# Folding a norm's weight vector into the weights of the first projection of a two-layer trunk, with the start written in another order

## The chip, the cores and the metric

The kernel runs on one core of a Trainium2 chip, as one launch. The metric is the device time of that launch in microseconds; smaller is better. TensorE (PE) multiplies, its weight loads have a row of their own (PEld); VectorE is DVE, ScalarE is ACT, GpSimd is POOL, and SyncE (SP) issues nearly all transfers.

## What is computed

Two residual layers on 256 tokens of width 1024, float32 in and out. Layer 0 mixes tokens with a matrix-memory mixer, layer 1 with block-sparse attention, and each is followed by a SwiGLU block. The change touches the norm ahead of the mixer of layer 0 and the projection that reads it:

```
def rmsnorm(x, g):
    y = xf * lax.rsqrt(jnp.mean(xf * xf, axis=-1, keepdims=True) + EPS)
    return (y * g.astype(F32)).astype(x.dtype)
...
u = rmsnorm(h, norm_mix[layer])
...
q, k, v, o, gl = jnp.split(u @ w_in, [sq, 2 * sq, 2 * sq + sv, 2 * sq + 2 * sv], axis=-1)
```

In layer 0 `w_in` has 1024 rows and 3080 columns: Q and K (512 each), V and O (1024 each) and 8 gate columns. `g` scales the 1024 features, so it can be applied to `u` or to the rows of `w_in`.

## The kernel before

**Two fp16 parts.** Every float32 operand is split into a high part (rounded to fp16) and a low part (what is left). A product is three fp16 matmuls: high by high, high by low, low by high (`proj_tok`). The high part of a weight is one ACT instruction (`wh`), the low part one DVE instruction that reads the raw weight and the high part (`wl`).

**Weights.** They stream in as 1 MB tiles `raw0`, `raw1`, ... (128 partitions by 2048 columns), in the order in which they are used: `raw0`, `raw1` hold the first half of V, `raw2`, `raw3` Q, `raw4`, `raw5` K, `raw6`, `raw7` the second half of V, `raw8` to `raw11` O, `raw12` to `raw15` the output projection, and from `raw16` on the SwiGLU block. There are 5 raw buffers and 8 buffers for the parts, so a load waits until DVE has made the low parts of the tile five before it. `Weights.high` and `Weights.low` split a half tile, 1024 columns, in one instruction each (lines 283 to 298).

**Who sets the order.** Each engine runs its instructions in the order in which the program issues them (`in_queue_order`). A planner, `Pace`, keeps an estimated clock; after each matmul step `Weights.ahead` may issue one more split of each kind if it thinks that ACT or DVE is free. Ahead of that, the first projection is issued by a table written out by hand, `START` (line 62), which `start_step` (line 537) executes: `square`, `rms` (norm factor and scaled x of one of the two token tiles), `flip` (four TensorE transposes of 128 columns into a PSUM bank), `uh` and `ul` (high and low part of the transposed x, four 128-column instructions each, with the norm's weight as the per-partition scale `gmix`), `wh` and `wl` (parts of one 512-column row chunk k of `raw0` or `raw1`), `v t k` (the three matmuls of token tile t with chunk k, tile `av`), and `ahead`, from where the planner may add splits.

**After V.** V's two banks are evacuated by ACT (`vah`) and DVE (`val`). Then Q is computed for both token tiles (`aq`, 24 matmuls each); each result is copied by ACT and DVE into `n`. Then the gates, a small product (`gate`), and a chain of small steps on ACT and DVE that ends in `lf`. TensorE meanwhile runs the 24 matmuls of K for tile 0 (`ak`), then the running sum of `lf` (`pf`), three more `ak`, and then the transpose `pr` of `acol`, which DVE makes from `pf` (`fcum`, `acol`). TensorE's order is fixed, so nothing behind `pr` can start before `acol` is there.

Of the kernel before, what the change touches and what calls it, by code (L numbers as in the profile page):

```python
# [16 lines left out]
ALU = mybir.AluOpType  # L17
# [42 lines left out]


START = [
    ("square", 0), ("rms", 0), ("flip", 0, 0), ("flip", 0, 1), ("square", 1), ("gain",), ("rms", 1), ("uh", 0, 0),
# [139 lines left out]
def trunk(ctx: ExitStack, tc: tile.TileContext, a: dict, out: bass.AP):  # L203
# [16 lines left out]
    def mm(dst, lhsT, rhs, start, stop):  # L220
        nc.tensor.matmul(dst, lhsT, rhs, start=start, stop=stop)  # L221
# [36 lines left out]
    class Weights:  # L258
# [18 lines left out]
            pace.work("DMA", 0.73)  # L277
            self.landed[i] = pace.end + 2.2

        def half(self, n):  # L280
            return slice(n % 2 * 1024, (n % 2 + 1) * 1024)

        def high(self):

            i, sl = self.highs // 2, self.half(self.highs)
            if i == len(self.parts):
                self.parts.append([wpool.tile([P, 2048], F16, tag=f"w{x}", bufs=WBUFS, name=f"w{x}{i}") for x in "hl"])
            nc.scalar.activation(self.parts[i][0][:, sl], self.raws[i][:, sl], AF.Copy, scale=WS)
            self.split[self.highs] = pace.end
            self.highs += 1  # L290

        def low(self):

            i, sl = self.lows // 2, self.half(self.lows)
            h, l = self.parts[i]
            nc.vector.scalar_tensor_tensor(l[:, sl], self.raws[i][:, sl], WS, h[:, sl], op0=ALU.mult, op1=ALU.subtract)
            self.lows += 1
            self.owed += 1 - self.lows % 2

# [117 lines left out]
        nc.gpsimd.tensor_tensor(r, s1, mhalf[:, 0:1], op=ALU.pow)  # L417
        return r

    def rms(name, t, ss, engine):  # L420

        r = rms_factor(ss)
        un = act.tile([P, D], F32, tag="u", name=f"u_{name}")
        for j in range(2):
            sl = slice(j * 512, (j + 1) * 512)
            engine.tensor_scalar(un[:, sl], hres[t][:, sl], r, 1.0, op0=ALU.mult, op1=ALU.mult)
        return un

    def gain_row(src):
# [32 lines left out]
    def split_cols(dh, dl, pt, gcols, k0, t, part):  # L462

        sl = slice(t * P, (t + 1) * P)
        for i in range(4):
            src, g, h = pt[:, i * P:(i + 1) * P], gcols[:, k0 + i:k0 + i + 1], dh[:, k0 + i, sl]
            if part == "uh":
                nc.scalar.activation(h, src, AF.Copy, scale=g)
            else:
                nc.vector.scalar_tensor_tensor(dl[:, k0 + i, sl], src, g, h, op0=ALU.mult, op1=ALU.subtract)  # L470

    def flip16(dst, src):

# [61 lines left out]
    un, pts = {}, {}  # L535

    def start_step(op, *i):
        if op == "gain":
            nc.vector.tensor_scalar(gmix, gb[:, 0:KD], math.sqrt(D) * AS, None, op0=ALU.mult)
        elif op == "square":  # L540
            square_half(1, i[0], ss[1])
        elif op == "rms":
            un[i[0]] = rms(f"a{i[0]}", i[0], ss[i[0]], (nc.vector, nc.gpsimd)[i[0]])
        elif op == "flip":
            pts[i] = ybank(f"ut_a{i[0]}{i[1]}")
            transpose4(pts[i], un[i[0]][:, i[1] * 512:(i[1] + 1) * 512])
        elif op in ("uh", "ul"):
            split_cols(*u[0:2], pts[i], gmix, 4 * i[1], i[0], op)
# [143 lines left out]
    for g in range(2):  # L692
        w = ws.take_k(2, 4)
        for t in range(NT):
# [507 lines left out]
```

## Time and profile before

| | |
|---|---|
| median of 3 runs | 553.78 us (553.05 to 554.00) |
| the profiled execution | 554.33 us |
| its span in the profile | 552.6 us |
| TensorE busy | 538.5 us, 97% |
| VectorE busy | 356.1 us, 64% |
| ScalarE busy | 309.1 us, 56% |

The profiled execution is 0.55 us over the median. Busy is the share of the span in which the engine had an instruction in flight; it does not tell the clock of TensorE, which has a row of its own.

### The profile page before, as it was taken

What the parts mean: (1) busy time and instruction counts of PE and PEld (TensorE: products, weight loads), DVE (VectorE), ACT (ScalarE), POOL (GpSimd) and SP (SyncE); (2) the same over time, 40 slices, a digit from 0 to 9 for tenths busy, and PEclk for the clock granted to TensorE, in tenths of its full rate; (3) what the DMA queues carried; (4) which work ended last, traced back from release to release, by engine and by line L of the source; (5) the groups of instructions that cost most, each with busy time, mean ns of one, the idle gap of its engine ahead of it and who ended that gap; (6) DMA issues with size and microseconds to landing.
All of it is one profiled execution on the core that took longest, in us unless ns stands there. A gap on an engine that the chain in (4) does not pass through costs nothing.

```text
span 552.6 us, 7773 instructions
## 1 busy us (share of the span) xinstructions
PE 538.5 (97%) x2650; PEld 251.3 (45%) x2650; DVE 356.1 (64%) x540; ACT 309.1 (56%) x548; POOL 46.0 (8%) x105
## 2 busy tenths in 40 slices
PE   7999999999999999999999999998999999999997
PEld 3454644444444444444444445543444444444443
DVE  3888798448766556682368898857566666575701
ACT  6867784358445445471348995836546455464600
POOL 4500160010300000000012220000000000000000
PEclk8999999999999999999999999999999999999999
DMA  8999969598599878892099979737879797889602
GB/s 304 362 288 239 360 172 288 131 204 227 154 237 249 220 219 247 256 390 96 3 257 338 284 180 256 137 86 225 226 212 258 194 262 219 215 242 306 236 0 78
DMA packets 140680, 122.34 MB, mean 221 GB/s; under 512 B 66472, under 2 KB 111536, under 8 KB 140640
## 3 DMA queue, kind: packets, MB, share of 16 engines
q1 hardware_dynamic: 139904, 119.58, 76.8%
q0 software_dynamic: 736, 2.27, 1.4%
q8 instruction: 21, 0.34, 0.3%
q14 instruction: 19, 0.16, 0.1%
HBM read 106.08 MB, written 1.05 MB: 194 GB/s over the span
## 4 chain that ended last, share of the span: by engine, by line
PE 89%; DMA 3%; issue 3%; ACT 2%; DVE 1%; POOL 1%; SPq 1%; ACTq 0%; POOLq 0%; DVEq 0%
PE gu L221 38%; PE f1o L221 10%; PE f0o L221 10%; PE b L221 7%; PE ao L221 6%; PE av L221 4%; PE bv L221 4%; PE bo L221 2%; DMA u_f<-n 2%; PE ak L221 2%; PE aq L221 2%; DMA raw<-in_ffn_w_in 1%; PE s L221 1%; PE num L221 1%; PE o L221 1%
## 5 line engine op out<-in xcount | busy, mean ns | idle before, releaser
L177 DVE SCALAR_TENSOR_TENSOR wl<-raw,wh 128x1024 f16<-128x1024 f32 (+1 forms) x200 | 236.6, 1203 | 38.4 <-ACT wh L177 36.3
L177 ACT ACTIVATE wh<-raw 128x1024 f16<-128x1024 f32 (+1 forms) x200 | 201.9, 1040 | 48.6 <-DMA raw<-in_ffn_w_out 22.4
L221 PE MATMUL gu<-wh,u_f 128*128 128x512 f16 x704 | 210.1, 379 | 4.3 <-DMA u_f<-n 4.3
L221 PEld LDWEIGHTS <-u_f 128*128 128x128 f16 x1056 | 103.0, 98 | 131.6 <-DMA u_f<-n 6.3
L221 PE MATMUL gu<-wl,u_f 128*128 128x512 f16 x352 | 133.4, 379 | 1.4 <-DVE wl L177 1.4
L221 PEld LDWEIGHTS <-h 128*128 128x128 f16 x528 | 51.7, 98 | 62.3
L177 DVE SCALAR_TENSOR_TENSOR fh<-gu,fsg 128x256 f32<-128x256 f32 x44 | 18.6, 423 | 54.2 <-ACT fsg L177 54.1
L177 ACT ACTIVATE fsg<-gu 128x256 f32<-128x256 f32 x44 | 16.8, 382 | 63.3 <-PE gu L221 63.3
L221 PE MATMUL f0o<-wh,h 128*128 128x512 f16 x176 | 46.6, 379 | 0.0
L221 PE MATMUL f1o<-wh,h 128*128 128x512 f16 x176 | 46.6, 379 | 0.0
L221 PEld LDWEIGHTS <-u_a 128*128 128x128 f16 x336 | 29.2, 99 | 34.9 <-ACT u_a L177 1.9
L221 PEld LDWEIGHTS <-u_b 128*128 128x128 f16 x288 | 27.8, 98 | 32.8 <-issue 1.0
L221 PE MATMUL b<-wh,u_b 128*128 128x512 f16 x128 | 38.9, 379 | 0.0
L177 ACT ACTIVATE junk<-x 128x512 f32<-128x512 f32 x16 | 10.1, 630 | 41.6 <-DVE x L177 39.3
L221 PE MATMUL f1o<-wl,h 128*128 128x512 f16 x88 | 27.5, 379 | 0.0
L221 PE MATMUL f0o<-wl,h 128*128 128x512 f16 x88 | 27.4, 379 | 0.0
L177 DVE TENSOR_TENSOR n<-fh,n 128x256 f16<-128x256 f32 x44 | 18.6, 422 | 10.7 <-ACT n L177 10.7
L221 PE MATMUL b<-wl,u_b 128*128 128x512 f16 x64 | 24.3, 379 | 0.7 <-DVE wl L177 0.7
L177 ACT ACTIVATE n<-fh 128x256 f16<-128x256 f32 x44 | 18.0, 409 | 11.9 <-DMA u_f<-n 5.9
L221 PE MATMUL av<-wh,u_a 128*128 128x512 f16 x64 | 21.8, 403 | 1.7 <-ACT u_a L177 1.7
L177 POOL TENSOR_TENSOR r<-s,mhalf 128x1 f32<-128x1 f32 x8 | 4.9, 609 | 212.9 <-DVE s L177 212.9
L221 PE MATMUL bv<-wh,u_b 128*128 128x512 f16 x64 | 20.0, 379 | 0.0
(178 smaller groups left out, 470.6 us busy)
## 6 DMA issues: line engine op xcount, KB each, us to landing
raw<-in_ffn_w_in SPq DMA_DIRECT2D x176, 256.0 KB, 4.4
raw<-in_ffn_w_out SPq DMA_DIRECT2D x88, 256.0 KB, 5.2
raw<-in_a_w_in SPq DMA_DIRECT2D x48, 256.0 KB, 5.4
raw<-in_b_w_in SPq DMA_DIRECT2D x48, 256.0 KB, 5.4
raw<-in_a_w_out SPq DMA_DIRECT2D x16, 256.0 KB, 5.7
raw<-in_b_w_out SPq DMA_DIRECT2D x16, 256.0 KB, 5.2
grow<-in_norm_ffn POOLq DMA_DIRECT2D x2, 512.0 KB, 6.6
out<-x SPq DMA_DIRECT2D x4, 256.0 KB, 2.1
```

The costliest lines, as they stand in the source:

```text
L177: return fn(*args, **kw)
L221: nc.tensor.matmul(dst, lhsT, rhs, start=start, stop=stop)
```

## The change

The scale `gmix` of the norm's weight leaves the split of x and enters the split of the weights. x is now split with a constant, so that one instruction covers 512 columns (4 x 128) where four did. Every weight tile of the layer's input projection (`raw0` to `raw11`) is split with `gmix[:, k]`, which differs from chunk to chunk, so a half tile of 1024 columns takes two instructions of 512 on ACT and two on DVE. The gate columns are multiplied by the gain first. The table `START` is written anew: token tile 0 goes first, six zero matmuls (`warm`) are put between the first steps, the scaling of token tile 1 moves from POOL to DVE, and `ahead` stands four steps of V from the end where it stood seven.

```
 START = [
-    ("square", 0), ("rms", 0), ("flip", 0, 0), ("flip", 0, 1), ("square", 1), ("gain",), ("rms", 1), ("uh", 0, 0),
+    ("square", 0), ("rms", 0), ("flip", 0, 0), ("flip", 0, 1), ("warm", 1), ("gain",), ("uh", 0, 0), ("wh", 0), ("ul", 0, 0), ("wl", 0),
...
-        def half(self, n):
-            return slice(n % 2 * 1024, (n % 2 + 1) * 1024)
+        def rows(self, n):
+
+            i, h = n // 2, n % 2 * 1024
+            if i >= 12:
+                return [(slice(h, h + 1024), WS)]
+            k = i % 2 * 4 + n % 2 * 2
+            return [(slice(h + j * 512, h + (j + 1) * 512), self.gains[:, k + j:k + j + 1]) for j in range(2)]
...
-            nc.scalar.activation(self.parts[i][0][:, sl], self.raws[i][:, sl], AF.Copy, scale=WS)
+            for sl, scale in self.rows(self.highs):
+                nc.scalar.activation(self.parts[i][0][:, sl], self.raws[i][:, sl], AF.Copy, scale=scale)
...
-            nc.vector.scalar_tensor_tensor(l[:, sl], self.raws[i][:, sl], WS, h[:, sl], op0=ALU.mult, op1=ALU.subtract)
+            for sl, scale in self.rows(self.lows):
+                nc.vector.scalar_tensor_tensor(l[:, sl], self.raws[i][:, sl], scale, h[:, sl], op0=ALU.mult, op1=ALU.subtract)
...
-            engine.tensor_scalar(un[:, sl], hres[t][:, sl], r, 1.0, op0=ALU.mult, op1=ALU.mult)
+            nc.vector.tensor_scalar(un[:, sl], hres[t][:, sl], r, 1.0, op0=ALU.mult, op1=ALU.mult)
...
-        for i in range(4):
-            src, g, h = pt[:, i * P:(i + 1) * P], gcols[:, k0 + i:k0 + i + 1], dh[:, k0 + i, sl]
-            if part == "uh":
-                nc.scalar.activation(h, src, AF.Copy, scale=g)
-            else:
-                nc.vector.scalar_tensor_tensor(dl[:, k0 + i, sl], src, g, h, op0=ALU.mult, op1=ALU.subtract)
+        h, l = (d[:, k0:k0 + 4, t * P:(t + 1) * P] for d in (dh, dl))
+        v = pt.rearrange("p (k n) -> p k n", k=4)
+        c = math.sqrt(D) * AS
+        if part == "uh":
+            nc.scalar.activation(h, v, AF.Copy, scale=c)
+        else:
+            nc.vector.scalar_tensor_tensor(l, v, c, h, op0=ALU.mult, op1=ALU.subtract)
...
-            nc.scalar.activation(w[k][0], raw, AF.Copy, scale=WS)
+            nc.scalar.activation(w[k][0], raw, AF.Copy, scale=gmix[:, k:k + 1])
...
-            nc.vector.tensor_scalar(gmix, gb[:, 0:KD], math.sqrt(D) * AS, None, op0=ALU.mult)
+            nc.vector.tensor_scalar(gmix, gb[:, 0:KD], WS, None, op0=ALU.mult)
+            ws.gains = gmix
+        elif op == "warm":
+            for _ in range(i[0]):
+                mm(warm, zero16[:, 0:P], zero16, True, True)
...
-                nc.vector.tensor_scalar(gh, gr, WS, None, op0=ALU.mult)
-                nc.vector.scalar_tensor_tensor(gl, gr, WS, gh, op0=ALU.mult, op1=ALU.subtract)
+                nc.vector.tensor_tensor(gr, gr, gmix.unsqueeze(2).to_broadcast([P, KD, 8]), op=ALU.mult)
+                nc.vector.tensor_copy(gh, gr)
+                nc.vector.tensor_tensor(gl, gr, gh, op=ALU.subtract)
```

What this does to the queues is seen at three places. The first is ACT from its first weight split to the second token tile, before and in the change (`u16_a` is the split x, `ut_a` the transposes, `junk` the squares of x).

```order
L177 ACTIVATE wh0_126<-raw0_88 128x512
L177 ACTIVATE junk_143,ss_133<-x1_84 128x512
L177 ACTIVATE junk_162,ss_133<-x1_84 128x512
L177 ACTIVATE u16_a_125<-ut_a00_152,cols_mix_141 128x128 x4
L177 ACTIVATE wh0_126<-raw0_88 128x512 x3
L177 ACTIVATE u16_a_125<-ut_a10_184,cols_mix_141 128x128 x4
```

```order
L177 ACTIVATE u16_a_125<-ut_a00_149 128x4x128
L177 ACTIVATE wh0_126<-raw0_88,cols_mix_136 128x512
L177 ACTIVATE u16_a_125<-ut_a01_154 128x4x128
L177 ACTIVATE wh0_126<-raw0_88,cols_mix_136 128x512
L177 ACTIVATE junk_174,ss_133<-x1_84 128x512
L177 ACTIVATE junk_176,ss_133<-x1_84 128x512
L177 ACTIVATE wh0_126<-raw0_88,cols_mix_136 128x512 x2
L177 ACTIVATE wh1_128<-raw1_94,cols_mix_136 128x512
L177 ACTIVATE u16_a_125<-ut_a10_201 128x4x128
```

The squares of token tile 1 have moved behind the first two weight chunks, and both halves of token tile 0 stand ahead of them. The second place is TensorE at the same point, as a difference: two `warm` matmuls take the place of the transposes of token tile 1, which now stand behind the fourth step of V.

```order
-L459 MATMUL ut_a_184<-ident,u_a_169 128x128 x4
-L459 MATMUL ut_a_189<-ident,u_a_169 128x128 x4
+L221 LDWEIGHTS zero_77
+L221 MATMUL warm<-zero_77 128x512
+L221 LDWEIGHTS zero_77
+L221 MATMUL warm<-zero_77 128x512
```

Behind the V product TensorE's instructions stand in the same order as before to the end. The third place is DVE from the evacuation of V to the copy of the second Q tile (`n16<-aq1`), before and in the change.

```order
L177 SCALAR_TENSOR_TENSOR wl2_270<-raw2_99,wh2_269 128x1024 x2
L177 SCALAR_TENSOR_TENSOR wl3_284<-raw3_104,wh3_283 128x1024
L177 SCALAR_TENSOR_TENSOR val_335<-av00_130,vah_334 128x512
L177 SCALAR_TENSOR_TENSOR val_335<-av01_131,vah_334 128x512
L177 SCALAR_TENSOR_TENSOR wl3_284<-raw3_104,wh3_283 128x1024
L177 SCALAR_TENSOR_TENSOR wl4_300<-raw4_109,wh4_299 128x1024 x2
L177 SCALAR_TENSOR_TENSOR n16_400<-aq0_358,n16_400 128x512
L177 TENSOR_SCALAR gh_347<-gr_305 128x64
L177 SCALAR_TENSOR_TENSOR gl_348<-gr_305,gh_347 128x64
L177 SCALAR_TENSOR_TENSOR wl5_381<-raw5_256,wh5_380 128x1024 x2
L177 SCALAR_TENSOR_TENSOR wl6_398<-raw6_261,wh6_397 128x1024
L177 SCALAR_TENSOR_TENSOR n16_445<-aq1_406,n16_445 128x512
```

```order
L177 SCALAR_TENSOR_TENSOR wl2_261<-raw2_99,cols_mix_136,wh2_260 128x512 x2
L177 SCALAR_TENSOR_TENSOR val_310<-av00_130,vah_309 128x512
L177 SCALAR_TENSOR_TENSOR val_310<-av01_131,vah_309 128x512
L177 SCALAR_TENSOR_TENSOR wl2_261<-raw2_99,cols_mix_136,wh2_260 128x512 x2
L177 SCALAR_TENSOR_TENSOR wl3_335<-raw3_104,cols_mix_136,wh3_334 128x512 x4
L177 SCALAR_TENSOR_TENSOR n16_381<-aq0_344,n16_381 128x512
L177 TENSOR_TENSOR gr_280<-gr_280,cols_mix_136 128x64
L177 CAST gh_322<-gr_280 128x64
L177 TENSOR_TENSOR gl_323<-gr_280,gh_322 128x64
L177 SCALAR_TENSOR_TENSOR wl4_367<-raw4_109,cols_mix_136,wh4_366 128x512 x4
L177 SCALAR_TENSOR_TENSOR wl5_398<-raw5_247,cols_mix_136,wh5_397 128x512 x4
L177 SCALAR_TENSOR_TENSOR n16_438<-aq1_388,n16_438 128x512
```

Three half tiles were split ahead of `val` before, one is now; between the two copies of Q there are four half tiles where there were three.

## Rows read from the trace of the kernel before

**Rows 1.** The page, its parts 1 and 2: TensorE's busy time, its granted clock

```profile
PE 538.5 (97%) x2650; PEld 251.3 (45%) x2650; DVE 356.1 (64%) x540; ACT 309.1 (56%) x548; POOL 46.0 (8%) x105
...
PEclk8999999999999999999999999999999999999999
```

**Rows 2.** Stretches of the start: length, busy us (instructions) per engine, PEclk, DMA share, GB/s

```profile
5.70:9.00 3.30, 1.56 (x10) 1.01 (x10) 1.01 (x4) 2.16 (x6) 0.16 (x1) 1.00 1.03 398
9.10:15.80 6.70, 6.45 (x18) 2.77 (x19) 5.84 (x17) 6.02 (x19) 6.37 (x12) 0.50 1.05 390
```

**Rows 3.** Timeline of the start, TensorE, POOL, DVE: start, us, instruction, [idle before <-releaser]

```profile
5.29 0.57 POOL L177 TENSOR_TENSOR r<-s,mhalf 128x1 f32<-128x1 f32 x1 [3.76 <-DVE s L177]
5.78 0.39 PE L221 MATMUL warm<-zero 128*128 128x512 f16 x1
5.89 0.88 DVE L177 TENSOR_SCALAR u_a<-x,r 128x512 f32<-128x512 f32 x2 [0.69 <-POOL r L177]
6.43 1.09 PE L459 MATMUL ut_a<-ident,u_a 128*128 128x128 f32 x8 [0.26 <-DVE u_a L177]
...
9.22 0.61 PE L221 MATMUL av<-wh,u_a 128*128 128x512 f16 x1 [1.70 <-ACT u_a L177]
...
24.22 0.38 PE L221 MATMUL aq<-wh,u_a 128*128 128x512 f16 x1
```

**Rows 4.** The chain that ended last, after V: start, us, what

```profile
24.39 10.36 PE aq L221 x48
```

**Rows 5.** Timeline of the weight loads of TensorE at `pr`

```profile
42.35 0.09 PEld L653 LDWEIGHTS pr<-ident,acol 128*4 128x4 f32 x2 [0.49 <-DVE acol L177]
```

**Rows 6.** Timeline of DVE from the evacuation of V to `acol`

```profile
25.05 1.29 DVE L177 SCALAR_TENSOR_TENSOR val<-av,vah 128x512 f16<-128x512 f32 x2 [1.63 <-ACT vah L177]
26.26 3.48 DVE L177 SCALAR_TENSOR_TENSOR wl<-raw,wh 128x1024 f16<-128x1024 f32 x3
30.23 0.69 DVE L177 SCALAR_TENSOR_TENSOR n<-aq,n 128x512 f16<-128x512 f32 x1 [0.49 <-ACT n L177]
...
31.20 3.49 DVE L177 SCALAR_TENSOR_TENSOR wl<-raw,wh 128x1024 f16<-128x1024 f32 x3
35.41 0.69 DVE L177 SCALAR_TENSOR_TENSOR n<-aq,n 128x512 f16<-128x512 f32 x1 [0.72 <-ACT n L177]
...
38.53 3.49 DVE L177 SCALAR_TENSOR_TENSOR wl<-raw,wh 128x1024 f16<-128x1024 f32 x3
41.94 0.16 DVE L177 COPY fcum<-pf 128x8 f32<-128x8 f32 x1
42.13 0.17 DVE L177 TENSOR_TENSOR acol<-gate,fcum 128x8 f32<-128x8 f32 x1
```

**Rows 7.** Timeline of ACT in the start

```profile
7.44 0.63 ACT L177 ACTIVATE junk<-x 128x512 f32<-128x512 f32 x1 [0.77 <-DMA x<-in_x]
...
8.82 1.12 ACT L177 ACTIVATE u_a<-ut_a,cols_mix 128x128 f16<-128x128 f32 x4
9.82 1.68 ACT L177 ACTIVATE wh<-raw 128x512 f16<-128x512 f32 x3
...
24.42 1.09 ACT L177 ACTIVATE vah<-av 128x512 f16<-128x512 f32 x2 [2.23 <-PE av L221]
```

**Rows 8.** Groups by form, whole span: constant or per-partition scale; xcount | busy us, mean ns

```profile
L177 DVE SCALAR_TENSOR_TENSOR u_f<-x,r,grow 128x512 f32<-128x512 f32 x4 | 2.8, 749 | 1.3 <-POOL r L177 1.3
...
L177 DVE SCALAR_TENSOR_TENSOR n<-u_f,n 128x512 f16<-128x512 f32 x4 | 2.7, 692 | 0.1
```

**Rows 9.** The same view for ACT

```profile
L177 ACT ACTIVATE n<-fh 128x256 f16<-128x256 f32 x44 | 18.0, 409 | 11.9 <-DMA u_f<-n 5.9 <-DVE fh L177 5.3 <-DMA h<-n 0.7
...
L177 ACT ACTIVATE p<-p,rsm 128x256 f16<-128x256 f32 x8 | 4.2, 530 | 0.0
```

**Rows 10.** TensorE's waits over the span: us in total, times, longest

```profile
PE gu L221 <- DMA u_f<-n: 4.3, 4, 1.9
PE av L221 <- ACT u_a L177: 1.7, 1, 1.7
```

More of the change, by code (lines that the diff above doesn't have):

```diff
@@ L278, in quarter @@
             self.landed[i] = pace.end + 2.2
-        def half(self, n):
-            return slice(n % 2 * 1024, (n % 2 + 1) * 1024)
+        def rows(self, n):
[4 more added lines that the diff above has]
+            return [(slice(h + j * 512, h + (j + 1) * 512), self.gains[:, k + j:k + j + 1]) for j in range(2)]
         def high(self):
-            i, sl = self.highs // 2, self.half(self.highs)
+            i = self.highs // 2
             if i == len(self.parts):
                 self.parts.append([wpool.tile([P, 2048], F16, tag=f"w{x}", bufs=WBUFS, name=f"w{x}{i}") for x in "hl"])
-            nc.scalar.activation(self.parts[i][0][:, sl], self.raws[i][:, sl], AF.Copy, scale=WS)
+            for sl, scale in self.rows(self.highs):
+                nc.scalar.activation(self.parts[i][0][:, sl], self.raws[i][:, sl], AF.Copy, scale=scale)
             self.split[self.highs] = pace.end
@@ L292, in low @@
         def low(self):
-            i, sl = self.lows // 2, self.half(self.lows)
+            i = self.lows // 2
             h, l = self.parts[i]
-            nc.vector.scalar_tensor_tensor(l[:, sl], self.raws[i][:, sl], WS, h[:, sl], op0=ALU.mult, op1=ALU.subtract)
+            for sl, scale in self.rows(self.lows):
+                nc.vector.scalar_tensor_tensor(l[:, sl], self.raws[i][:, sl], scale, h[:, sl], op0=ALU.mult, op1=ALU.subtract)
             self.lows += 1
@@ L418, in rms_factor, with rms @@
         return r
-    def rms(name, t, ss, engine):
-        r = rms_factor(ss)
+    def rms(name, t, r):
         un = act.tile([P, D], F32, tag="u", name=f"u_{name}")
@@ L460, in transpose4, with split_cols @@
         pace.spend(0.44)
-    def split_cols(dh, dl, pt, gcols, k0, t, part):
-        sl = slice(t * P, (t + 1) * P)
-        for i in range(4):
-            src, g, h = pt[:, i * P:(i + 1) * P], gcols[:, k0 + i:k0 + i + 1], dh[:, k0 + i, sl]
-            if part == "uh":
-                nc.scalar.activation(h, src, AF.Copy, scale=g)
-            else:
-                nc.vector.scalar_tensor_tensor(dl[:, k0 + i, sl], src, g, h, op0=ALU.mult, op1=ALU.subtract)
+    def split_cols(dh, dl, pt, k0, t, part):
+        h, l = (d[:, k0:k0 + 4, t * P:(t + 1) * P] for d in (dh, dl))
[5 more added lines that the diff above has]
+            nc.vector.scalar_tensor_tensor(l, v, c, h, op0=ALU.mult, op1=ALU.subtract)
     def flip16(dst, src):
@@ L523, in split_chunk @@
         if op == "wh":
-            nc.scalar.activation(w[k][0], raw, AF.Copy, scale=WS)
+            nc.scalar.activation(w[k][0], raw, AF.Copy, scale=gmix[:, k:k + 1])
         else:
-            nc.vector.scalar_tensor_tensor(w[k][1], raw, WS, w[k][0], op0=ALU.mult, op1=ALU.subtract)
+            nc.vector.scalar_tensor_tensor(w[k][1], raw, gmix[:, k:k + 1], w[k][0], op0=ALU.mult, op1=ALU.subtract)
     ss = [new_ss(t) for t in range(NT)]
-    for n in range(2):
-        square_half(0, n, ss[0])
-    split_chunk(0, "wh")
     gb, gmix = gain_cols("mix", rows_mix, KD)
@@ L534, in trunk @@
         mm(warm, zero16[:, 0:P], zero16, True, True)
-    un, pts = {}, {}
+    un, pts, factor = {}, {}, {}
     def start_step(op, *i):
         if op == "gain":
-            nc.vector.tensor_scalar(gmix, gb[:, 0:KD], math.sqrt(D) * AS, None, op0=ALU.mult)
+            nc.vector.tensor_scalar(gmix, gb[:, 0:KD], WS, None, op0=ALU.mult)
[3 more added lines that the diff above has]
+                mm(warm, zero16[:, 0:P], zero16, True, True)
         elif op == "square":
-            square_half(1, i[0], ss[1])
+            for n in range(2):
+                square_half(i[0], n, ss[i[0]])
         elif op == "rms":
-            un[i[0]] = rms(f"a{i[0]}", i[0], ss[i[0]], (nc.vector, nc.gpsimd)[i[0]])
+            factor[i[0]] = rms_factor(ss[i[0]])
+            if i[0] == 0:
+                un[0] = rms("a0", 0, factor[0])
+        elif op == "scale":
+            un[1] = rms("a1", 1, factor[1])
         elif op == "flip":
@@ L547, in start_step @@
         elif op in ("uh", "ul"):
[L548 removed]
+            split_cols(*u[0:2], pts[i], 4 * i[1], i[0], op)
         elif op in ("wh", "wl"):
```

10 rows, old and new, of the table START are left out of this document.

## The prediction, made before the changed kernel had run

> **What bounds the kernel.** I read the page first: TensorE is busy for 97% of the span, and only the first of its 40 slices shows a clock under full speed [rows 1]. A time saved elsewhere is therefore worth nothing unless TensorE waits for it, and whatever TensorE gains or loses at one place it carries to the end, as long as nothing later absorbs it. Next I read its waits: there are few, the longest 1.9 us on the transposed norm of a SwiGLU block, and 1.7 us in the start for the split of x [rows 10]. Then the start itself. The zero matmul at 5.78 takes 0.39 us and the granted clock is 1.00 until 9.0; TensorE then stands still from the transposes (6.43 to 7.52) to 9.22, and from 9.1 to 15.8 it is granted half, 1.2 GHz [rows 2, 3]. So the V product runs cold for two thirds of its time and the first matmul of Q comes at 24.22 [rows 3]. From there 48 matmuls of Q take 10.36 us, 0.216 each, with no wait [rows 4], and TensorE goes on so past `pr`. That is the place to look at: the weight load of `pr` waited 0.49 us for `acol` and got it just as the matmuls ahead of it ended [rows 5]. DVE's queue thus already arrives at 42.35 with no slack, though TensorE does not yet stand still for it.
>
> **The start.** Prices: an ACT instruction of 512 columns out of PSUM takes 0.60 and the next starts after 0.49 (two in 1.09), a weight chunk of 512 after 0.53 (three in 1.68) [rows 7]. The chunk now has a per-partition scale. On ACT a 256-column instruction with one takes 530 ns, one with a constant 409 [rows 9]; I take 0.10 more per instruction, 0.63 from start to start, because the two rows differ by 0.12 but read different tiles. The Trainium skill (ScalarE: Activation LUTs, What ACT_TABLE_LOAD costs) says that each per-partition pointer operand adds about 93 ns, which speaks against the change; by it the five pointer splits ahead of the second token tile would cost 0.03 us less in all than by my 0.10.
>
> The first four transposes are done at about 7.05 (half of 1.09 from 6.43, and the tail) [rows 3]. ACT then runs: `uh` 7.05 to 7.65, first chunk to 8.3, `uh` to 8.8, second chunk to 9.4, the two squares of tile 1 (1.38 from 7.44 to the next instruction at 8.82 [rows 7]) to 10.8, third chunk to 11.4, fourth to 12.05. DVE follows: third low part 11.5 to 12.15, then the scaling of tile 1 (its factor is ready at 11.7, after POOL's 0.57; two instructions take 0.88 [rows 3]) to 13.0, fourth low part to 13.7. TensorE finishes the fourth step of tile 0 at 14.15 and transposes tile 1; the first half is there at 14.75, its high part at 15.4, its low part at 16.15, the step that needs it ends at 16.4. Eleven steps of three matmuls at 0.216 follow: V ends at 23.5 where it ended at 24.22. **Gain of the start: 0.7 us.** The six zero matmuls, 1.3 us at full clock, lie in gaps in which TensorE waits for the splits; without that cover they would cost 1.3. The clock moves this sum less than it seems, since up to the fourth step TensorE waits for splits at either clock. If it stayed at half from 9.1 to 15.8 as before, the last two matmuls of that step would cost 0.4 more and the transposes 0.5, and V would end at 24.4; I take full clock and keep this for the upper end.
>
> **After V.** Here the change takes more than it gave. Prices on DVE: 512 columns with a constant, 0.605 from start to start (`val`: two from 25.05 to 26.26); 1024 columns, 1.137 (three from 38.53 to 41.94) [rows 6]. A per-partition scale: 749 against 692 ns at 512 columns [rows 8], so 0.06 more, 0.665 per new split and 1.33 per half tile. No row shows this very form. From below the scale could be free, 0.605; from above it could cost what it does on ACT, 0.12 [rows 9], so 0.725. I take 0.665, since rows 8 are the same engine and size.
>
> `val` started 0.83 after Q's first matmul (25.05 against 24.22) because the last step of V was tile 0's; now tile 0 ends one step, 0.65, earlier. So `val` starts at 23.5 + 0.18 = 23.7. Behind it stand two halves of `raw3`'s and one of `raw2`'s low parts that Q itself needs, six splits: 23.7 + 1.21 + 6 x 0.665, and 0.08 for the last one's end, gives 28.98. TensorE, at Q since 23.5, cannot run its last step of tile 0 before that; two more matmuls end at 29.46. Before, 24 of them ended at 24.22 + 5.18 = 29.40. **The gain of the start is gone at the end of the first Q tile.** DVE's copy of it comes 0.84 later as before (30.23 against 29.40 [rows 6]): 30.30. From its start to the next split 0.97 us went by (30.23 to 31.20); a third small gate instruction makes it 1.17 (0.2, as from `fcum` to `acol` [rows 6]). With 8 x 0.665 = 5.32 the copy of the second Q tile starts at 36.79. Before it started at 35.41, after 0.72 of idling. All the small gate steps stand behind it, 3.12 us from there to 38.53 [rows 6]; then six splits, 3.99, where three of 1024 took 3.41. `acol` is 1.38 + 0.58 = **2.0 us later** than before, at about 44.1. TensorE reaches `pr` at the same time as before and now waits for it. Everything behind stands in the same order, so TensorE carries the 2.0 to the end.
>
> Check of the other parts. ACT has 20 splits of 0.63 between the first `val` and `pr`, 12.6 us of some 20, and each high part is needed only when DVE comes to it, at 0.665 apiece; I count nothing. Transfers: the buffer of `raw2` comes free at 26.3 and no longer ahead of `val`, so `raw7` is loaded later, but its second half is split only behind `pr`. There 18 splits, to the end of `raw11`, cost DVE 0.1 us more each than half of a 1024-column one, 1.7 us in all. TensorE has moved 2.0 back by then, and I count nothing for it; if that cover is gone, it costs up to 1.7 where the scores of the heads wait for DVE. The scaling of tile 1 leaves POOL, which nobody waits for afterwards.
>
> **Sum.** -0.7 in the start, +2.7 from there to `pr`: +2.0. Against the profiled execution, 554.33, that is 556.3; that execution was 0.55 over the median of the runs, so I forecast **555.8 us** for the median.
>
> **Rivals.** (1) The DVE queue keeps up, and the change is faster. It needs `acol` 1.1 us earlier than before. Even with V at 23.0 and the first `val` at 23.2 that is 2.6 us less from there than I count, or 20 splits at 0.54 instead of 0.665. The bare rate of the columns is 1.137 - 0.605 = 0.53 per 512, so the fixed part and the scale would both have to vanish; that is the point from which it decides. For it speaks that rows 8 are not weight splits; against it, `val`. Its time is that of the start's gain with V ending between 23.0 and 23.5: 0.7 to 1.2 less, 552.6 to 553.1. Chance 0.12. (2) DVE is late, but less: a free scale and V at 23.0 (ACT's scale free too) give 0.5 less for `val` and 20 x 0.06 less behind it, `acol` 0.3 late: 554.1; with 1.0 late, 554.8. Chance 0.23. (3) The clock or a second wait adds to it. The clock fell after a gap of 1.7 us once, and stayed low for 6.7 us [rows 2, 3]. If it does that again where TensorE transposes tile 1 or stands at `pr`, half a stretch of that length costs 1.7 more: 557.5. Against it: the wait of 1.9 us on the norms [rows 10] left the clock at full [rows 1]. Or DVE, dearer by 1.7 up to `raw11`, holds up the heads. Chance 0.15. (4) The forecast, 554.9 to 557: chance 0.50.
>
> **How the numbers follow.** A measurement of this kernel can tell about 0.2%, 1.1 us, from no change: 552.7 to 554.9. Faster: rival 1, 0.12. The same: rival 2, 0.23. Slower: the forecast and rival 3, 0.65. The range leaves out most of rival 1 and the end of rival 3: **553.0 to 557.8**. The forecast's own range is 554.9 to 557.
>
> **What would show it.** In the changed profile: V ends near 23.5 with no stretch, or a shorter one, at half clock; a 512-column low part of `raw2` or later at about 0.665 from start to start; TensorE waits of a few tenths in Q's first tile for `wl`; the copy of the second Q tile on DVE behind `wl` and not behind ACT; a TensorE wait of about 2 us at `pr` for `acol`, which is a new row among its waits; the remaining waits as before. I am wrong if `pr` waits for nothing, if DVE's splits come at 0.57 or less, or if V ends before 22.5.

## The result, and the profile after

| | before | changed |
|---|---|---|
| median | 553.48 us (5 executions, 552.44 to 554.00) | 557.41 us (5 executions, 556.15 to 558.64) |
| ratio | | 1.0076, 95% interval 1.0054 to 1.0099 |
| the profiled execution, its span | 554.33, 552.6 us | 556.15, 554.2 us |

The change makes the kernel slower, by 0.5 to 1.0% (by 0.3 to 0.7% when it was measured again, experiment 1). Between the two profiled executions the difference is 1.8 us, between the medians 3.9; where the rest comes from is told below. The page, parts 1 and 2, of the changed kernel:

```profile
PE 537.9 (97%) x2656; PEld 251.0 (45%) x2656; DVE 360.5 (65%) x551; ACT 313.7 (57%) x556; POOL 43.3 (8%) x103
...
PEclk9999999999999999999999999999999999999999
```

TensorE's busy time is the same [rows 1]; the first of the 40 slices now shows full clock. In the stretches of the start:

```profile
5.70:9.00 3.30, 2.50 (x12) 1.40 (x13) 2.12 (x5) 1.79 (x4) 0.16 (x1) 1.00 1.02 366
9.10:15.80 6.70, 5.13 (x24) 2.37 (x23) 4.14 (x8) 4.17 (x10) 4.43 (x10) 1.00 1.05 387
```

The half clock of the second stretch [rows 2] is gone, yet TensorE is less busy there: it waits. The timeline of the start and of `pr` (start, us, instruction, [idle before <-releaser]):

```profile
6.44 1.17 PE L465 MATMUL ut_a<-ident,u_a 128*128 128x128 f32 x8
...
11.60 0.75 DVE L177 SCALAR_TENSOR_TENSOR wl<-raw,cols_mix,wh 128x512 f16<-128x512 f32 x1 [0.40 <-ACT wh L177]
11.79 1.11 POOL L580 DMA_DIRECT2D gr<-in_a_w_in  x1
12.27 1.24 DVE L177 TENSOR_SCALAR u_a<-x,r 128x512 f32<-128x512 f32 x2
13.44 0.74 DVE L177 SCALAR_TENSOR_TENSOR wl<-raw,cols_mix,wh 128x512 f16<-128x512 f32 x1
14.22 0.38 PE L221 MATMUL av<-wl,u_a 128*128 128x512 f16 x1 [0.80 <-DVE wl L177]
14.65 1.03 PE L465 MATMUL ut_a<-ident,u_a 128*128 128x128 f32 x8
...
16.53 0.96 DVE L177 SCALAR_TENSOR_TENSOR wl<-raw,cols_mix,wh 128x512 f16<-128x512 f32 x1
16.67 0.60 PE L221 MATMUL av<-wh,u_a 128*128 128x512 f16 x2
...
24.02 0.38 PE L221 MATMUL aq<-wh,u_a 128*128 128x512 f16 x1
...
26.25 0.38 PE L221 MATMUL aq<-wl,u_a 128*128 128x512 f16 x1 [0.56 <-DVE wl L177]
...
44.95 0.38 PE L665 MATMUL pr<-ident,acol 128*4 128x128 f32 x2 [2.00 <-DVE acol L177]
```

V ends at 24.02, only 0.2 earlier than before [rows 3]. TensorE waits 0.56 in Q's first tile for a low part and 2.00 at `pr`, where before had no wait at either place. The queue that it waits for is DVE's:

```profile
24.20 1.34 DVE L177 SCALAR_TENSOR_TENSOR val<-av,vah 128x512 f16<-128x512 f32 x2 [2.38 <-ACT vah L177]
25.46 4.06 DVE L177 SCALAR_TENSOR_TENSOR wl<-raw,cols_mix,wh 128x512 f16<-128x512 f32 x6
30.83 0.69 DVE L177 SCALAR_TENSOR_TENSOR n<-aq,n 128x512 f16<-128x512 f32 x1 [1.31 <-ACT n L177]
...
32.05 5.38 DVE L177 SCALAR_TENSOR_TENSOR wl<-raw,cols_mix,wh 128x512 f16<-128x512 f32 x8
37.35 0.68 DVE L177 SCALAR_TENSOR_TENSOR n<-aq,n 128x512 f16<-128x512 f32 x1
...
40.47 4.06 DVE L177 SCALAR_TENSOR_TENSOR wl<-raw,cols_mix,wh 128x512 f16<-128x512 f32 x6
44.45 0.16 DVE L177 COPY fcum<-pf 128x8 f32<-128x8 f32 x1
44.64 0.17 DVE L177 TENSOR_TENSOR acol<-gate,fcum 128x8 f32<-128x8 f32 x1
```

Against [rows 6]: six splits stand between `val` and the first copy, eight between the copies, with no idling ahead of the second copy, and `acol` comes 2.5 later. The 2.38 us that DVE idles ahead of `val` are no relief, because the splits that are missing later stand behind `val`. The groups by form, and TensorE's waits over the span (us in total, times, longest):

```profile
L177 DVE SCALAR_TENSOR_TENSOR wl<-raw,cols_mix,wh 128x512 f16<-128x512 f32 x48 | 33.5, 758 | 0.4 <-ACT wh L177 0.4
...
L177 ACT ACTIVATE wh<-raw,cols_mix 128x512 f16<-128x512 f32 x48 | 30.6, 715 | 0.0
```

```profile
PE gu L221 <- DMA u_f<-n: 3.3, 3, 1.8
PE pr L665 <- DVE acol L177: 2.0, 1, 2.0
...
PE aq L221 <- DVE wl L177: 0.6, 1, 0.6
```

The bill: `pr` runs 2.6 us later (44.95 against 42.36, which is 0.01 behind the weight load of [rows 5]), but the span is only 1.6 longer. The missing 1.0 is the wait that left the first row: three waits of 3.3 us where [rows 10] had four of 4.3. It is this one of the kernel before, on the norm of layer 0's SwiGLU block, shown with SyncE's two transposes that it waits for:

```profile
111.67 6.58 SPq L474 DMA_TRANSPOSE u_f<-n  x2
...
119.32 0.39 PE L221 MATMUL gu<-wh,u_f 128*128 128x512 f16 x1 [1.05 <-DMA u_f<-n]
```

In the changed kernel the same two transposes take 1.05 less, and TensorE does not wait:

```profile
114.27 5.53 SPq L480 DMA_TRANSPOSE u_f<-n  x2
```

The other part of the median's difference is the clock. Of the changed kernel's twelve executions in this and the next run, the eight with a mean granted clock of 0.999 or 1.00 took 555.64 to 557.10, the four with 0.996 or 0.997 took 557.41 to 558.64.

### The profile page after: what moved, and what is told of

Same layout as the page of the kernel before. It is cut to its first block, busy times and chain, and to the rows that moved or that the text cites. A ratio compares the mean times of both kernels' runs of the same rounds, so it can differ in the third digit from the quotient of the medians.

```text
span 554.2 us, 7778 instructions
## 1 busy us (share of the span) xinstructions
PE 537.9 (97%) x2656; PEld 251.0 (45%) x2656; DVE 360.5 (65%) x551; ACT 313.7 (57%) x556; POOL 43.3 (8%) x103
## 3 DMA queue, kind: packets, MB, share of 16 engines
HBM read 106.08 MB, written 1.05 MB: 193 GB/s over the span
## 4 chain that ended last, share of the span: by engine, by line
PE 85%; DMA 5%; DVE 4%; issue 2%; ACT 2%; SPq 1%; POOL 0%; DVEq 0%; ACTq 0%; POOLq 0%
PE gu L221 37%; PE f1o L221 10%; PE f0o L221 10%; PE b L221 7%; PE ao L221 6%; PE bv L221 4%; PE av L221 3%; PE bo L221 2%; DVE wl L177 2%; DMA u_f<-n 2%; DMA x<-in_x 1%; DMA raw<-in_ffn_w_in 1%; PE s L221 1%; PE ak L221 1%; PE num L221 1%
## 5 line engine op out<-in xcount | busy, mean ns | idle before, releaser
L177 DVE SCALAR_TENSOR_TENSOR wl<-raw,wh 128x1024 f16<-128x1024 f32 x172 | 207.5, 1221 | 36.5 <-ACT wh L177 34.4
L177 ACT ACTIVATE wh<-raw 128x1024 f16<-128x1024 f32 x172 | 178.6, 1059 | 47.3 <-DMA raw<-in_ffn_w_in 25.5
L177 DVE SCALAR_TENSOR_TENSOR wl<-raw,cols_mix,wh 128x512 f16<-128x512 f32 x48 | 33.5, 758 | 0.4 <-ACT wh L177 0.4
L177 ACT ACTIVATE wh<-raw,cols_mix 128x512 f16<-128x512 f32 x48 | 30.6, 715 | 0.0
```

The source lines that it names most:

```text
L177: return fn(*args, **kw)
```

## The experiments

The kernels ran in three groups (experiments 1 to 4, 5 to 8 and 9 to 12), each beside the kernel before on the same chip, whose medians were 553.82, 553.93 and 553.66 us (30, 23 and 35 executions). Two stretches of each profiled execution tell the kernels apart better than the whole time does: from the first transposes to Q's first matmul (A), and from there to `pr` (B). Where `pr` was moved back, six matmuls are 1.3 us and nine 1.9 us of B. B repeats: it is 20.92 or 20.93 in the five profiles that have the changed kernel's splits in their places (the changed kernel twice, experiments 2, 8 and 12). A repeats less well, because the clock falls in some starts: the fold alone and the fold with `pr` later have the same start and differ by 0.77.

| kernel | median, us (executions) | ratio to before, 95% | A | B | waits in B |
|---|---|---|---|---|---|
| before | 553.48 (5) | | 17.79 | 18.14 | none |
| changed | 557.41 (5) | 1.0054 to 1.0099 | 17.58 | 20.93 | 0.56, 2.00 |
| changed, again | 556.25 (7) | 1.0028 to 1.0068 | 17.50 | 20.93 | 0.6, 1.99 |
| `pr` nine matmuls later | 555.18 (12) | 1.0008 to 1.0039 | 17.88 | 20.92 | 0.6 |
| 1024 columns, constant | 554.74 (12) | 1.0011 to 1.0042 | 17.84 | 19.44 | 1.03 |
| 512 columns, constant | 555.20 (12) | 1.0018 to 1.0049 | 17.55 | 19.94 | 0.5, 1.15 |
| fold alone | 553.82 (12) | 0.9992 to 1.0023 | 16.75 | 18.98 | 0.84 |
| order alone | 556.62 (6) | 1.0031 to 1.0067 | 18.61 | 19.36 | 1.03 |
| low parts of Q earlier | 554.38 (12) | 0.9996 to 1.0026 | 17.42 | 19.19 | 1.04 |
| no zero matmuls | 558.17 (6) | 1.0056 to 1.0102 | 17.72 | 20.93 | 0.6, 1.99 |
| fold, `pr` later | 553.21 (12) | 0.9970 to 1.0006 | 17.52 | 19.27 | none |
| fold, zero matmuls, `pr` later | 553.22 (12) | 0.9954 to 0.9998 | 16.52 | 19.27 | none |
| low parts earlier, `pr` later | 554.64 (12) | 0.9988 to 1.0030 | 17.81 | 19.28 | none |
| POOL's DMA issues later | 556.93 (12) | 1.0025 to 1.0065 | 17.31 | 20.92 | 0.6, 1.99 |

**1. The changed kernel again.**

> The changed kernel once more, unchanged, for a second trace beside the runs below. If the time lost is a queue of fixed length on DVE, the wait of TensorE for acol at pr is 2.0 us again within 0.2, and the time lies between 556 and 559. If the spread of the five runs seen (556.2 to 558.6) is TensorE's clock, this trace shows a stretch at half clock in the start or behind pr whenever its time is over 557; if it is the transposes of the norm ahead of the SwiGLU block, it shows a wait of about 1 us for u_f at the second token tile, which the first trace of this kernel did not have.

A, B and both waits come back to within 0.1 us, and the wait at `u_f` is missing again. Only one of its seven executions had the lower clock, which fits the median, 1.2 us lower. Where the slower executions lose their time this run could not tell, since the profiled one took 556.27.

**2. `pr` later**: `"cm"`, the planner's delay ahead of `pr`, 5.47 to 7.6.

> Only pr moves: nine matmuls of K (1.9 us) later in TensorE's order. Theory, DVE's queue is late at acol: TensorE has work in that time, the wait of 2.0 us at pr shrinks to under 0.2, and the time falls by 1.8 to 2.0 against the changed kernel. Rival, the wait only moves (to the mask of the decay or to the heads behind): a new wait of 1 to 2 us further on and the same time within 0.5. Rival, TensorE's clock falls because of the stand at pr: the time falls by 3 or more, and no run has a clock under 0.999.

B is the same 20.92 with nine matmuls of K more in it: the 2.00 us at `pr` are filled with work. The wait was thus a real stop and not work that would have been done anyway. Of the executions at 0.999 or 1.00 the median is 554.5 (7), against 556.2 of the eight of the changed kernel: 1.7 of the 2.0 come through. Between the medians of all executions it is 1.1, because five of the twelve had a clock of 0.996 or 0.997, with no wait at `pr`. The profiled execution was one of these (557.31). It lost some 1.7 us behind the norm of layer 1, where the clock falls to half from the matmul on that follows a wait of 1.95 us (0.67 over the four microseconds shown, 0.90 over the next four):

```profile
388.00:392.00 4.00, 2.82 (x8) 1.02 (x8) 2.25 (x5) 2.37 (x4) 0.00 (x0) 0.67 0.96 226
```

In the changed kernel's own profile the wait there is 1.85 and the clock stays at 1.00. In the start of this profile, too, TensorE is slow: its matmuls take 0.57 to 0.63 us up to 10.06, where the changed kernel's take 0.38, although the granted clock reads 1.00 there.

**3. and 4. The price of a split, in two steps.** Both leave the norm's weight out of Q, K, O and the second half of V. The third splits these tiles in 1024 columns with a constant, the fourth in 512 with a constant:

```
-            if i >= 12:
+            if i >= 2:
```

```
-            return [(slice(h + j * 512, h + (j + 1) * 512), self.gains[:, k + j:k + j + 1]) for j in range(2)]
+            return [(slice(h + j * 512, h + (j + 1) * 512), WS) for j in range(2)]
```

> From raw2 on, the weights are split as before the change: one instruction of 1024 columns with a constant; this leaves the gain out of Q, K, O and the second half of V. The new START stays. Theory, DVE's queue: 20 splits at 0.665 become 10 at 1.137, 1.9 us less up to acol; the wait at pr is 0.3 or less, Q's first tile waits less, and the time is 1.5 to 2 us under the changed kernel. Rival, the new order of the start is what costs: the wait at pr stays over 1.5 us and the time changes by less than 0.5.

> From raw2 on, 512 columns per split as in the changed kernel, but with a constant in place of the gain (the gain is left out of Q, K, O and the second half of V). It parts the two prices: the scale, 0.06 per split by the rows, and the second instruction. Theory: a split takes 0.605 from start to start, 20 of them 1.2 us less, the wait at pr is 0.8 and the time 1.2 under the changed kernel. If the scale is free, the wait stays at 2.0; if the scale is all of the price, it falls by 1.9.

In the fourth, DVE's order is that of the changed kernel, and only the scale differs (timeline of DVE, the six splits ahead of `acol`, and ACT's group of splits):

```profile
39.91 3.69 DVE L177 SCALAR_TENSOR_TENSOR wl<-raw,wh 128x512 f16<-128x512 f32 x6
43.52 0.16 DVE L177 COPY fcum<-pf 128x8 f32<-128x8 f32 x1
...
L177 ACT ACTIVATE wh<-raw 128x512 f16<-128x512 f32 x40 | 21.7, 620 | 0.1
```

3.61 for six is 0.602 a split, against (44.45 - 40.47) / 6 = 0.663 in the changed kernel: the per-partition scale costs DVE 0.061 us. The fourteen splits behind the first copy make 0.85 of it, and the wait at `pr` falls by 0.85, from 2.00 to 1.15; I had expected 0.8, from all twenty splits, but ahead of the first copy DVE idles in both kernels. With 1024 columns the rest goes as well, but TensorE then waits 1.03 in Q's first tile, not less than 0.56 as I had it, since three half tiles of low parts that Q needs still stand behind `val`. So the price of the split explains the wait at `pr`, and not the whole of B: 1.3 of the 2.8 us are left at the old price.

**5. and 6. Either half alone.** The fold with the start in the old order (tile 1 scaled on POOL, no zero matmuls); and the new order without the fold (x split in four instructions with the scale, weights in 1024 columns with a constant):

```
+    ("square", 0), ("rms", 0), ("flip", 0, 0), ("flip", 0, 1), ("gain",), ("wh", 0), ("square", 1), ("rms", 1), ("scale", 1), ("uh", 0, 0),
+    ("wl", 0), ("ul", 0, 0), ("v", 0, 0), ("flip", 1, 0), ("flip", 1, 1), ("wh", 3), ("wh", 1), ("wh", 2),
...
+            un[1] = rms("a1", 1, factor[1], nc.gpsimd)
```

```
-            if i >= 12:
+            if i >= 2:
...
+        for i in range(4):
+            src, g, h = pt[:, i * P:(i + 1) * P], gcols[:, k0 + i:k0 + i + 1], dh[:, k0 + i, sl]
```

> The fold of the norm's weight and the 512-column splits alone; the start keeps the order of before (no zero matmuls among its steps, tile 1 scaled on POOL, the first weight chunk's high part behind the weight vector that it now needs). My theory (the price is DVE's: 20 splits with a per-partition scale between Q's first matmul and the weight load of pr): the last step of V is tile 0's again, so val starts some 0.8 us behind Q's first matmul as in before, but every 512 columns cost 0.66 where 1024 cost 1.14, so acol is late and TensorE waits at pr, by 0.6 to 1.5 us, since before had 0.49 and 0.72 us of idle DVE to use up; time 0.3 to 1.0 us over before. Rival, the order of the start is what costs: no wait at pr, time within 0.3 us of before or below it.

> The new order of the start alone: zero matmuls among its steps, tile 1 scaled on DVE, V's steps in the new order; the gain stays in the columns of x (four 128-column instructions) and the weights are split in 1024 columns with a constant. My theory: with four small instructions per half of x instead of one, V ends about 1 us later than in the changed kernel, 24.7 to 25.5; val comes early behind Q's first matmul, so that the second tile of low parts stands in front of nothing at pr: wait at pr 0 to 0.3, a wait of up to 1 us in Q's first tile for a low part; time 554.5 to 555.8, 1 to 2 over before, from the start. Rival, the order of the start is what the wait at pr comes from (val ahead of the second half tiles): a wait of 1 us or more at pr with 1024-column splits too, time over 556.

Stretch of the start and timeline of TensorE, the fold alone:

```profile
9.10:15.80 6.70, 6.00 (x23) 2.87 (x23) 5.63 (x9) 5.78 (x12) 6.03 (x11) 0.75 1.05 391
...
23.14 0.38 PE L221 MATMUL aq<-wh,u_a 128*128 128x512 f16 x1
...
42.12 0.38 PE L665 MATMUL pr<-ident,acol 128*4 128x128 f32 x2 [0.84 <-DVE acol L177]
```

and the order alone:

```profile
9.10:15.80 6.70, 5.48 (x21) 2.26 (x20) 5.14 (x13) 4.09 (x11) 3.72 (x8) 0.75 1.05 391
...
25.01 0.38 PE L221 MATMUL aq<-wh,u_a 128*128 128x512 f16 x1
...
27.72 0.38 PE L221 MATMUL aq<-wl,u_a 128*128 128x512 f16 x1 [1.03 <-DVE wl L177]
...
44.37 0.38 PE L665 MATMUL pr<-ident,acol 128*4 128x128 f32 x2
```

The fold alone costs nothing (553.82 against 553.93): it pays 0.84 at `pr`, as my theory had it, but V ends earlier, which I had not counted, and `pr` runs 0.24 sooner than before. Two things go with the earlier end of V, and no run takes them apart: the shorter split of x, and a clock that is at half for a shorter time (0.75 on average over the stretch of [rows 2], where before has 0.50). The order alone gives nearly the whole loss, 556.62 against 553.93: A is 0.8 longer, then 1.03 in Q's first tile for a low part behind `val`. Its profile, too, has 0.75 in that stretch. At most 0.4 of the 0.8 is the clock's, since the low part that the fourth step needs is ready only at 14.62 and its matmul ran at 15.01; and its two executions with a clock of 0.999 or 1.00 still took 555.88. The rival's wait at `pr` did not come: there the order alone has none. Its wait is the one in Q's first tile. Summed over A and B of these profiles, against before: fold -0.2, order +2.0, both +2.6; with the A of 17.52 that the same start has in experiment 9, the fold would be +0.6, so that the sum is good to some 0.8 only. In these profiles the rest, 0.7, lies in B: the dearer splits cost 0.84 there in the old order and 1.57 in the new one, with more of them behind `val`.

**7. The low parts of Q earlier.** The parts of V's last two chunks stand ahead of tile 0's fifth step, and the planner may begin eight steps of V before the end (not seven, as the expectation below says) instead of four:

```
-    ("wl", 5), ("v", 0, 4), ("v", 1, 3), ("v", 1, 4), ("wh", 6), ("wl", 6), ("v", 0, 5), ("v", 1, 5), ("wh", 7), ("wl", 7),
-    ("ahead",), ("v", 0, 6), ("v", 1, 6), ("v", 0, 7), ("v", 1, 7),
+    ("wl", 5), ("wh", 6), ("wl", 6), ("wh", 7), ("wl", 7), ("v", 0, 4), ("ahead",), ("v", 1, 3), ("v", 1, 4), ("v", 0, 5), ("v", 1, 5),
+    ("v", 0, 6), ("v", 1, 6), ("v", 0, 7), ("v", 1, 7),
```

> The changed kernel with one thing moved: the high and low parts of V's last two chunks stand earlier in the start, and the step that starts Q's low parts stands seven steps of V ahead of the end instead of four, so DVE has three half tiles of low parts done before val (it idled 2.38 us there) and six splits instead of eight between the two copies of Q. My theory (DVE's queue behind val is what costs, and its order decides, not the price of a split): the wait of 0.56 in Q's first tile is gone, the wait at pr falls from 2.0 to between 0 and 0.7, time 1.3 to 2.5 us under the changed kernel at the same clock, 553.8 to 555.0. Rival, the price of the splits alone decides, wherever they stand: the wait at pr stays above 1.3 and the time within 0.7 us of the changed kernel's.

Timelines of DVE and TensorE:

```profile
24.14 1.28 DVE L177 SCALAR_TENSOR_TENSOR val<-av,vah 128x512 f16<-128x512 f32 x2
...
42.97 0.38 PE L665 MATMUL pr<-ident,acol 128*4 128x128 f32 x2 [1.04 <-DVE acol L177]
```

DVE's idling ahead of `val` is gone, and so are the wait in Q's first tile and half of that at `pr` (more is left than the 0.7 that I expected at most). With the same number of splits at the same price B falls by 1.7, and the kernel is level with before. The rival, that the price alone decides wherever the splits stand, falls.

**8. No zero matmuls** among the steps of the start (the four `warm` entries of the table taken out).

> The changed kernel without the six zero matmuls between the steps of the start. My theory: they lie in TensorE's waits, so taking them out gives back no time in itself, but TensorE then stands still between the first transposes and the first step of V and again for the splits, and the granted clock falls to half there as it did in before (9.1 to 15.8); V ends 0.5 to 1.0 us later (24.5 to 25.0), the wait at pr shrinks by as much as DVE is early, so that the time moves by 0 to 0.6 us only. Rival 1: the clock stays at full without them, V ends within 0.2 of 24.02, no change in time. Rival 2: they stand in TensorE's way, V ends earlier by 0.2 or more.

My theory was wrong and the first rival right for the start: the clock stays at full there and A is 17.72, so in this profile the zero matmuls neither cost nor gave anything. The time is not lower, though. The profile has half clock at another place, right behind the wait at `pr`:

```profile
44.00:46.00 2.00, 0.89 (x6) 0.53 (x7) 1.21 (x5) 2.00 (x4) 0.00 (x0) 1.00 0.49 187
46.00:50.00 4.00, 4.00 (x12) 1.48 (x11) 3.80 (x9) 2.13 (x4) 0.00 (x0) 0.57 0.55 113
```

The changed kernel, with the same wait:

```profile
44.00:46.00 2.00, 1.05 (x6) 0.60 (x7) 1.20 (x4) 2.00 (x4) 0.00 (x0) 1.00 0.51 192
46.00:50.00 4.00, 4.00 (x20) 1.85 (x19) 3.80 (x9) 2.04 (x5) 0.00 (x0) 1.00 0.57 118
```

Twelve matmuls in four microseconds instead of twenty are 8 x 0.216 = 1.7 us. Five of the six executions had a mean clock of 0.993 to 0.996; the one at 0.999 took 555.56. Five of six against four of twelve of the changed kernel is too few to say that the zero matmuls make such a fall rarer.

**9. to 11. A better version.** `"cm"` at 6.6 puts `pr` six matmuls later: on the fold with the old order, on the same with eight zero matmuls behind the first transposes, and on the seventh kernel.

```
-    ("square", 0), ("rms", 0), ("flip", 0, 0), ("flip", 0, 1), ("gain",), ("wh", 0), ("square", 1), ("rms", 1), ("scale", 1), ("uh", 0, 0),
+    ("square", 0), ("rms", 0), ("flip", 0, 0), ("flip", 0, 1), ("warm", 8), ("gain",), ("wh", 0), ("square", 1), ("rms", 1), ("scale", 1), ("uh", 0, 0),
```

> The fold with the old order of the start, and pr and the step behind it six matmuls of K further back on TensorE (1.3 us). My theory: the 0.84 us that TensorE stood at pr in the fold alone was DVE's queue of 512-column splits and nothing else, so it goes; pr then runs at 42.6 without a wait, and the time is 0.5 to 0.9 under that of the fold alone, 552.9 to 553.4, under before. Rival: what TensorE gains is given back at the transposed norm of layer 0 (the wait of 1.05 for u_f at 119 that before has and the fold alone has not), or at the heads: 553.6 to 554.2.

> As the run with the fold, the old order and the later pr, and eight zero matmuls (1.7 us) behind the first transposes, where TensorE stands still for 2.2 us. My theory: the granted clock then stays at full between 10 and 13.5, where it is half in the fold alone; the three matmuls of V and eight transposes there take 1.4 us less, but DVE has no more than 0.9 us of idle time between 9 and V's end, so V ends 0.3 to 0.9 earlier, at 22.2 to 22.8, and the time is 0.2 to 0.8 less than without the zero matmuls. Rival: the clock falls later instead, at a wait further on (pr, or the transposed norm of layer 1 near 388), in more of the executions than before: the median is no better or up to 1.5 us worse.

> The run with the earlier start of Q's low parts, and pr six matmuls of K further back. My theory: the wait of 1.04 us at pr goes as well, 0.6 to 1.0 less than without it, 553.4 to 553.9: no slower than before, but not faster, because V still ends 0.6 later than with the old order of the start. Rival: the wait moves to the next step for which TensorE waits on DVE (a wl of K or O): no change, 554.2 to 554.6.

In all three nothing waits in B. With the zero matmuls (timeline of TensorE):

```profile
7.51 1.89 PE L221 MATMUL warm<-zero 128*128 128x512 f16 x8
9.99 0.39 PE L221 MATMUL av<-wh,u_a 128*128 128x512 f16 x1 [0.59 <-ACT u_a L177]
...
22.92 0.38 PE L221 MATMUL aq<-wh,u_a 128*128 128x512 f16 x1
...
42.19 0.38 PE L665 MATMUL pr<-ident,acol 128*4 128x128 f32 x2
```

```profile
9.10:15.80 6.70, 5.20 (x26) 2.29 (x24) 5.77 (x9) 6.26 (x13) 5.83 (x9) 1.00 1.05 390
```

The wait of 2.2 us of the fold alone has become one of 0.59, the clock stays at full where the fold alone has 0.75 on average, and A is the shortest of all. This version's ratio to before is 0.9976 (0.9954 to 0.9998). That is the best ratio of the twelve kernels tried, its interval only just leaves out no change, and its median is that of the fold with the later `pr` (553.22 and 553.21), so that it is faster than before is not firmly shown. Both sides of its expectation came true: the six executions at 0.999 or 1.00 have a median of 552.1, the other six one of 554.4. The fold with the later `pr` alone can't be told from before. The third came out no better than without the later `pr` (554.64 against 554.38), although the wait is gone; at 0.999 or 1.00 it is 553.9 (7 executions) against 554.4 (10), so something was probably gained, and five executions with the lower clock hid it; the two ran in different groups.

**12. POOL's DMA issues later**: `gr`, `bgate` and `gout` are fetched behind the masks, not beside the scaling of tile 1.

```
-    nc.gpsimd.dma_start(gr, wa[:, GCOL:].rearrange("(k p) n -> p k n", p=P))
...
     nc.gpsimd.memset(zrow, 0.0)
+    nc.gpsimd.dma_start(gr, wa[:, GCOL:].rearrange("(k p) n -> p k n", p=P))
```

> The changed kernel with three DMA issues of POOL (gr, bgate, gout) moved behind its masks, so that they no longer stand beside the scaling of tile 1 on DVE (1.24 us instead of the 0.88 that I counted). My theory: it is the DMA issue that slows DVE; the scaling takes 0.88 to 0.95, V ends 0.3 to 0.4 earlier, 23.6 to 23.75, val and acol with it, the wait of 2.0 at pr stays as it is and the time is 0.3 to 0.4 less at the same clock. Rival: any work of POOL on its memory (memsets and masks, which now stand there) slows DVE as much: 1.1 or more, V's end at 24.0, no change.

```profile
12.27 0.94 DVE L177 TENSOR_SCALAR u_a<-x,r 128x512 f32<-128x512 f32 x2
...
23.75 0.38 PE L221 MATMUL aq<-wh,u_a 128*128 128x512 f16 x1
...
44.67 0.38 PE L665 MATMUL pr<-ident,acol 128*4 128x128 f32 x2 [1.99 <-DVE acol L177]
```

The scaling takes 0.94 with three of POOL's masks beside it, where it takes 1.20 to 1.25 in all nine profiles that have POOL's DMA issues there, so it was the issues that slowed it. V's end and `pr` come 0.27 earlier, a little less than expected. In the time this can't be seen (at 0.999 or 1.00 the median is 556.1 against 556.2): six of its twelve executions had the lower clock, and the profiled one shows it from 46 on, at 0.59 until 50, as without the zero matmuls.

## Why the prediction was right, and which terms were off

**Right: the place, the queue and the price.** The 0.665 us from split to split was measured as 0.663, and experiment 4 shows the scale's part of it, 0.061 against my 0.06. `val` follows V's end by 0.18, as counted. Six, eight and six splits stand where I put them, the copy of the second Q tile has no idling ahead of it, and TensorE waits 2.00 us at `pr` where I had "a TensorE wait of about 2 us". From V's end to `pr` it lost 2.8; I had 2.7. Behind V, ACT was not in the way; its scale cost 715 - 620 = 95 ns per instruction of 512 columns (the 620 from experiment 4), beside my 0.10. The Trainium skill (ScalarE: Activation LUTs, What ACT_TABLE_LOAD costs) puts each pointer operand at about 93 ns, and the trace agrees.

**Mis-sized: "Gain of the start: 0.7 us".** It was 0.2. The step that failed is the scaling of tile 1, "two instructions take 0.88". I took that from tile 0, where nothing ran beside it; here POOL issued DMAs at the same time and it took 1.24. From its start to the fourth low part it is 13.44 - 12.27 = 1.17 where I had 0.85, so 0.32 of the 0.5 is its own. Another 0.12 is its late start (12.27 where I had 12.15), and 0.04 the fourth low part (0.74 where I had 0.7). The transposes moved back by the sum, to 14.65 where I had 14.15, and experiment 12 gave 0.27 of it back. Behind them nothing more was lost: the `wl` at 16.53 is long, 0.96 us, beside POOL's `sel`, but from 16.67 to Q's first matmul TensorE runs its 34 matmuls at 0.216 each without a wait. That the clock would stay at full held in the changed kernel's two profiles.

**Not foreseen: 1.0 us came back behind `pr`.** "Everything behind stands in the same order, so TensorE carries the 2.0 to the end" held for the order and not for the waits. The wait of 1.05 at 119.32 is not in the changed kernel. It hardly comes back anywhere: of the other twelve profiles one has 0.70 there, one 0.33, the rest nothing, whether `pr` is late or early. It is therefore not the lateness that pays for it. The wait goes with the length of SyncE's two transposes: 6.58 us in the kernel before, 5.75 in the profile with the 0.70, and 4.96 to 5.63 in the others. What made them slow isn't settled; there is one profile of the kernel before, and whether its other executions have the wait is not known.

**Rival 3 was a part of the truth.** I gave 0.15 to the clock's falling again, at `pr` among other places, for 557.5. Two kernels with the changed kernel's wait show just this in their profiles, 1.7 us of it, and the median of the first five executions of the changed kernel is 557.41. In its own two profiles the clock stays up, so where its slower executions lost it is not shown; with `pr` nine matmuls later, and no wait there, five of twelve had the lower clock too. My argument against this rival, that the wait of 1.9 us on the norms leaves the clock at full, held in the profile of before; in experiment 2 the clock is at 0.67 behind a wait of 1.95.

**The number was in part luck.** The profiled execution, 556.15, lies near my sum for it, 556.3, because two errors had opposite signs: 0.5 too much gain in the start, and 1.0 that came back behind `pr`. My forecast for the median, 555.8, was too low both times, by 1.6 (557.41) and by 0.5 (556.25), and the first lies above the forecast's own range, 554.9 to 557: three of its five executions had a clock of 0.997.

**A reading that was wrong.** The V product did not run "cold for two thirds of its time": half clock from 9.1 to 15.8 covers 6.6 of its 15.0 us [rows 2, 3], well under half. The sum does not use it.

**What I had not taken apart.** I charged the loss to the dearer splits and to the early `val` together. Alone, the fold is free and the order costs about 2 us. 1.2 of them lie in B: the table of the start put two more half tiles of the low parts that Q needs behind `val`, while DVE idled ahead of it. The other 0.8 lies in A, up to half of it by the clock.

## What to carry to other kernels

When an order is written by hand for one engine, read what it does to the engine that is next to be full: filling the 2.4 us that DVE idled ahead of `val` took 1.7 us off the way to `pr`, 20 us later. Test the halves of a change apart before giving it up; here one half cost nothing by itself and the other made the loss. A stop of about 2 us on TensorE can cost twice, once for itself and once for the clock behind it: here 2.0 and, in some executions, 1.7.

## What the runs showed of the hardware

- A DVE scaling of 2 x 512 float32 columns took 0.88 us alone, 0.94 beside POOL's masks and 1.24 while POOL issued DMAs.
- After the same wait of 2.0 us at `pr` the granted clock stayed at 1.00 in two profiles and fell to half in two others. In the start it stayed up in the changed kernel with and without the zero matmuls (waits of up to 1.0 us), and fell behind the waits of 1.7 us (before) and 2.2 us (the fold alone), but also behind two of 1.09 and 0.87 us in the order alone. In experiment 2, with the changed kernel's start, the matmuls were at half rate up to 10.4 us.
- Every kernel whose profile shows full clock in the start also had executions of 1.3 to 2.7 us more (difference of medians) with a mean clock of 0.993 to 0.997. The kernel before, whose clock falls in the start, has slower ones too: 15 of its 88 show 0.990 or 0.991 and took 555.21 to 557.63. Where the clock fell was seen at `pr` and behind the norm of layer 1 (389 us); why in one execution and not in the next stays open.
